# The rows of 14 of 16 experts fetched by an indirect DMA from a copy of x in HBM, and the next gate product set between up and down

## The chip, the core and the metric

The kernel runs on one core of a Trainium2 chip. The metric is the time of one execution in device microseconds (us); the median of three runs stands for the kernel. The core's engines work side by side, each through its own list of instructions in order: TensorE (PE in the profile, with its weight loads as PEld) does matrix products and transposes, VectorE (DVE) and ScalarE (ACT) work on rows of 128 partitions, GpSimd (POOL) does a little of the same and can issue DMAs whose addresses come from a tile, SyncE (SP) issues the plain loads. An engine whose next instruction waits for a semaphore holds up everything behind it in its list.

## What is computed

An encoder of two layers on 512 tokens of 1024 channels, all in float32. A layer adds the outputs of four mixers to x, then those of a mixture of 16 experts in which each expert chooses its own 64 tokens:

```python
def expert_choice_moe(x, w_router, w_gate, w_up, w_down):
    b, L, d = x.shape
    cap = EC_CAPACITY * L // N_EXPERTS
    aff = jax.nn.softmax((x @ w_router).astype(F32), axis=-1)
    gate, idx = lax.top_k(jnp.swapaxes(aff, 1, 2), cap)
    xe = jax.vmap(lambda xb, ib: xb[ib])(x, idx)
    hdn = jax.nn.silu(jnp.einsum("becd,edf->becf", xe, w_gate)) * jnp.einsum("becd,edf->becf", xe, w_up)
    ye = jnp.einsum("becf,efd->becd", hdn, w_down) * gate[..., None].astype(x.dtype)
    return jax.vmap(lambda ib, yb: jnp.zeros((L, d), yb.dtype).at[ib.reshape(-1)].add(yb.reshape(-1, d)))(idx, ye)
...
        x = x + mix @ w_out[l]
        x = x + expert_choice_moe(rmsnorm(x, norm_ffn_w[l]), router_w[l], moe_w_gate[l],
                                  moe_w_up[l], moe_w_down[l])
```

The change lies in this last line alone, the "expert stage" below, which runs once in each layer.

## The kernel before

x lies in SBUF as four tiles of 128 tokens (`xrow(t)`). The three matrices of an expert are 1024 by 1024 float32, 4 MB each, 201 MB in a layer. They come as pieces of 512 KB (8 for a matrix), issued by SP in the order gate, up, down (`pieces`, L1351) into the slots of several tile pools that are used in turn (`ring`); a piece is issued once the product that read the slot's last piece is done, so SP waits for PE as well as for old DMAs. Some 40 pieces are there when the stage begins.

For each expert `ranks` transposes the 512 affinities onto every partition (`er`, L1278) and counts on DVE for each token how many are above it (`egt`, four instructions, L1282). `choose` (L1290, four on DVE) turns the ranks into a 0/1 matrix `eselr` of 512 tokens by 64 places, scaled by one over the root of the token's mean square. `expert_tokens` multiplies that matrix with x on PE (`ex`, L1301: 8 instructions, 16 matmul records in the trace since a float32 instruction leaves two), copies the result on ACT (`exe`, L1304), transposes it (`exT`, L1308, and DVE L1310, where the norm's weight is put on), builds the unscaled matrix `esel` on DVE (L1313) and from it the 64 gate values (`ers`, L1317, and DVE `erg`, L1320).

The products are `eg` and `eu` (gate and up: `exT` against the weights), and `ey` (down), all on L1359, 16 instructions or 32 records each. The hidden rows are silu(`eg`) on ACT (`eh`, L1406) times `eu` on DVE (L1409); they are transposed on PE (`ehT`, L1415) and copied by ACT (L1417), which `ey` waits for. ACT and DVE scale `ey` by the gate in two parts (`eY`, L1428 and L1429). Once for every two experts, `combine` puts the 128 rows back in their places by a product with the transposed choice (`eoT`, L1374, `eot` on ACT, `ec`, L1385) and adds them into new tiles of x (L1387).

The code is written expert by expert: `eg`, `eu`, then the next expert's rows (`prep`), `ehT`, `ey`, `combine`. A scheduler then sets the order on each engine, so that neighbouring steps can be mixed.

Of the kernel before, what the change touches and what calls it, by code (L numbers as in the profile page):

```python
# [20 lines left out]
P = 128  # L21
# [14 lines left out]
C_ID, C_LE, C_GE, C_IOTA, C_N = 0, 128, 256, 384, 448  # L36


def shape_constants():
# [6 lines left out]
    c[:, C_IOTA:C_IOTA + 64] = np.arange(1, 65)  # L46
    same = (p[:, None] // 32) == (p[None, :] // 32)
# [4 lines left out]
    # times n = c + 4 j of the classes c; frequencies w = 2 pi (f + 1/2) / 2 L, f < 128, stand for four:  # L52
    # w, pi - w, pi / 2 - w, pi / 2 + w
# [52 lines left out]
def encoder(ctx: ExitStack, tc: tile.TileContext, d, out, dbg=None, stages=None, nlayers=NL):  # L106
# [44 lines left out]
    def slots_in_order():  # L151
        """The tiles of a tag take their slots in program order."""
        last, seen = {}, set()
        for ins in list(nc.cur_bb.bb.instructions):
            for o in ins.outs:
                ap = getattr(o, "bass_ap", None)
                n = ap.tensor.name if ap is not None else None
                if n in made and n not in seen:
                    seen.add(n)
                    tag = made[n]  # L160
                    if tag in last and last[tag] is not ins:
                        no_sync(ins, last[tag], "slots in program order")
                    last[tag] = ins
# [16 lines left out]
    # ---------------------------------------------------------------- constants  # L180
# [38 lines left out]
    def masks():  # L219
# [5 lines left out]
        # of tokens of the same affinity the earlier one goes first: a bound for differences, by place  # L225
# [4 lines left out]
    # ------------------------------------------------- per-channel parameters  # L230
# [59 lines left out]
    def squares(ss, x, junk, both=False):  # L290
        """Sums of squares of the halves of a row into ss."""
# [8 lines left out]
    def row_rstd(ss, name):  # L300
        """One over the roots of the mean squares of the rows of ss."""
# [68 lines left out]
    def proj_cm(hT, raw, c, pool=False):  # L370
        """128 columns from c of raw, channels on partitions -> PSUM bank [128, 512]."""
# [10 lines left out]
    def proj_tm(l, hT, pieces, use, pool=False, raws=()):  # L382
        """Columns of pieces [(c0, n)], tokens on partitions; use(t, psum bank)."""
# [26 lines left out]
    def weave(*streams):  # L410
        """Emits streams (weight, generator) side by side, each yield being a part of the weight."""
# [14 lines left out]
    def silu_inplace(x, e, dst):  # L426
        """x: clamped at FLOOR; e: scratch of the same shape; dst = x*sigmoid(x)."""
# [10 lines left out]
    def mix_put(m, i, src, w=None):  # L438
        """src: [128 channels, 512] of mixer m, tile i, scaled by column w."""
# [8 lines left out]
    # ------------------------------------------------------------------- hyena  # L448
# [32 lines left out]
    def filter_hidden(cols, spec, zT, ws, w3, fb):  # L481
        """The first layer's spectrum; what the second's is made of (on partitions 64..) into scratch. A generator."""
# [32 lines left out]
    def filter_spec(spec, h, w3, fb, dec, kt):  # L515
        """The spectrum of a layer's filters into spec. A generator."""
# [14 lines left out]
        # sp[:, m, i]: frequencies w and pi - w (f = 0), pi / 2 - w and pi / 2 + w (f = 1); i: real part and  # L531
        # imaginary part, the latter with the other sign for pi - w and pi / 2 - w
# [57 lines left out]
    def hyena(l, st, spec):  # L590
# [4 lines left out]
        # cosine and sine sums of the classes; of those the spectra (xs as the filters', sine sums)  # L595
# [17 lines left out]
        def quarter(lo, hi, b):  # L613
            """lo = hi turned forth by b, hi = hi turned back; cosine and sine parts."""
# [16 lines left out]
        # what gives the samples of the classes  # L631
# [23 lines left out]
    # ------------------------------------------------------------------- mamba  # L655
# [45 lines left out]
    def mamba(l, st, bc, cols):  # L701
# [29 lines left out]
        # the cumulative sums in three exact bfloat16 parts, transposed: row 8*t + c of a part  # L731
# [35 lines left out]
        # states of the chunks and their scan  # L767
# [30 lines left out]
        # C B^T of every chunk, transposed; one bank for each group  # L798
# [78 lines left out]
    # --------------------------------------------------------------- attention  # L877
# [130 lines left out]
    # ------------------------------------------------------------------- HGRN2  # L1008
# [28 lines left out]
    def hgrn_values(v):  # L1037
        """The values of a chunk of 32 tokens, alone in the chunk's columns among those of 64 tokens."""
# [60 lines left out]
    def hgrn(l, st, cols, lb):  # L1099
# [25 lines left out]
                # R[:, n, c]: the state after chunk c (in the direction's order)  # L1125
# [60 lines left out]
    # ------------------------------------------------------------------ output projection  # L1186
# [10 lines left out]
    def out_part(t, n, js, W):  # L1197
        """Channel tiles js [(mixer, k)] of the mixers into the rows t, columns of half n."""
# [17 lines left out]
    def out_last(l, m, W):  # L1216
        """The first channel tile of mixer m; the halves of its weights into W. A generator."""
# [8 lines left out]
    # ------------------------------------------------------- expert choice MoE  # L1226
# [9 lines left out]
    def router(rw, st):  # L1236
        pl = bank_b("rl")
        plv = pl[:, :64].rearrange("p (t e) -> p t e", t=4)
        ra = small([4, 1 + NE], "ra")
        mx = small([4], "rmx")  # L1240
        den = small([4], "rden")
        for t in range(4):
# [12 lines left out]
            for k in range(8):  # L1255
                T.matmul(plv[:, t], xs[k // 4][:, k % 4], rw[:, k], start=(k == 0), stop=(k == 7))
            V.reduce_max(mx[:, t:t + 1], plv[:, t], axis=AX.X)
            V.tensor_scalar(ra[:, t, 1:], plv[:, t], mx[:, t:t + 1], None, op0=ALU.subtract)
# [5 lines left out]
            rsqrt(ra[:, t, 0:1], ss[:, 0:1], D, "ffn")  # L1264
            A.activation(ra[:, t, 1:], ra[:, t, 1:], AF.Exp, scale=ra[:, t, 0:1], accum_out=den[:, t:t + 1])
            V.reciprocal(den[:, t:t + 1], den[:, t:t + 1])
            V.tensor_scalar(ra[:, t, 1:], ra[:, t, 1:], den[:, t:t + 1], KEY, op0=ALU.mult, op1=ALU.mult)
# [3 lines left out]
    SELR = (V, V, V, V)  # L1271

    def ranks(e, ra, selr=None):
        """The ranks of the tokens, from one, by their affinity to expert e. The affinities are scaled by KEY:
        the difference of two that are not the same is then above TIE."""
        pr = bank_b("er")
        for t in range(4):
            T.transpose(pr[:, t * P:(t + 1) * P], ra[:, t, 1 + e:2 + e].to_broadcast([P, P]), ident)  # L1278
        rk = small([4], "erk", bufs=2)
        g = page([L], "egt", BF)  # L1280
        for c in range(4):
            V.scalar_tensor_tensor(g, pr, ra[:, c, 1 + e:2 + e], tie[:, 384 - c * P:896 - c * P],  # L1282
                                   op0=ALU.subtract, op1=ALU.is_gt, accum_out=rk[:, c:c + 1])
            if selr is not None:
                choose(selr, rk, ra, c, SELR[c])
# [6 lines left out]
    def expert_tokens(e, ra, nw, rk, sel, selr):  # L1292
        """The 64 tokens of expert e: their normed rows, transposed, and their gates; their choice into sel."""
        if selr is None:
            selr = page([4, 64], "eselr")
            for t in range(4):
                choose(selr, rk, ra, t, V)
        px = bank_b("ex")
        for t in range(4):
            for h in range(2):  # L1300
                T.matmul(px[64 * h:64 * h + 64], selr[:, t], xrow(t)[:, h * 512:(h + 1) * 512],  # L1301
                         start=(t == 0), stop=(t == 3))
        xe = page([L], "exe")
        A.activation(xe, px, AF.Copy)  # L1304
        yield
        pt = bank_b("exT")
        for j in range(4):
            T.transpose(pt[:, j * P:(j + 1) * P], xe[:, j::4], ident)  # L1308
        xeT = page([4, 2, 64], "exT")
        V.tensor_mul(xeT, pt.rearrange("p (j h s) -> p j h s", j=4, h=2), nw[:, :, :, None].to_broadcast([P, 4, 2, 64]))  # L1310
# [8 lines left out]
        gate = small([1], "erg", bufs=2)  # L1319
        V.tensor_scalar(gate, pr[:, :1], 1.0 / KEY, None, op0=ALU.mult)  # L1320
        yield xeT, gate

    # pieces of the experts' matrices go round the slots of all the tags
# [5 lines left out]
    def pieces(l, view):  # L1329
        """A generator: loads one piece after the other."""  # L1330
        spare = []
        for e in range(NE):
            for m in ("gate", "up", "down"):
                rows = d["moe_w_" + m][l, e].rearrange("(h p j) f -> h p j f", h=2, p=P)
                v = view[e, m] = []
# [214 lines left out]
```

## Time and profile before

| what | value |
|---|---|
| three runs | 1733.29 to 1740.3 us, median 1737.68 us |
| span of the profiled execution | 1732.9 us |
| median less span | 4.8 us |
| PE busy | 1643.3 us, 95% of the span |
| weights' and other plain loads (queue q1) | 455.10 MB |
| expert stage, first layer | first `eg` at 372 us, last `ey` ends at 861 us |
| expert stage, second layer | first `eg` at 1225 us, last `ey` ends at 1714 us |

The profile shows one execution of one core; what lies around its span can only be seen from the median, 4.8 us. The two expert stages are 489 us each, 56% of the span together, and look alike, so one of them is read here and counted twice. A matmul's end is modelled, so that a busy PE need not be at its peak; idle time of an engine that nobody waits for costs nothing.

### The profile page before, as it was taken

What the parts mean: (1) busy time and instruction counts of PE and PEld (TensorE: products, weight loads), DVE (VectorE), ACT (ScalarE), POOL (GpSimd) and SP (SyncE); (2) the same over time, 40 slices, a digit from 0 to 9 for tenths busy, and PEclk for the clock granted to TensorE, in tenths of its full rate; (3) what the DMA queues carried; (4) which work ended last, traced back from release to release, by engine and by line L of the source; (5) the groups of instructions that cost most, each with busy time, mean ns of one, the idle gap of its engine ahead of it and who ended that gap; (6) DMA issues with size and microseconds to landing.
All of it is one profiled execution on the core that took longest, in us unless ns stands there. A gap on an engine that the chain in (4) does not pass through costs nothing.

```text
span 1732.9 us, 23297 instructions
## 1 busy us (share of the span) xinstructions
PE 1643.3 (95%) x9155; PEld 935.1 (54%) x9155; DVE 812.5 (47%) x1785; ACT 421.7 (24%) x849; POOL 166.8 (10%) x158
## 2 busy tenths in 40 slices
PE   7989999989999999999989999899999999999996
PEld 6778777754344333433368787787343343334332
DVE  6677776642334233233165767856332333233233
ACT  4343424321011111111252444344111011111103
POOL 3132131000000000000033223300000000000001
PEclk9989999999999999999989889999999999999998
DMA  5411126659999999999413111286699999999981
GB/s 171 112 49 50 50 73 237 254 210 375 381 409 411 410 411 410 411 407 396 143 50 97 50 42 57 74 308 231 234 376 411 411 411 410 411 411 408 409 329 49
DMA packets 150959, 457.03 MB, mean 264 GB/s; under 512 B 19928, under 2 KB 56184, under 8 KB 142658
## 3 DMA queue, kind: packets, MB, share of 16 engines
q1 hardware_dynamic: 145606, 455.10, 68.4%
q8 instruction: 72, 1.18, 0.3%
q10 hardware_dynamic: 5244, 0.45, 0.2%
q14 instruction: 37, 0.30, 0.1%
HBM read 453.25 MB, written 2.24 MB: 263 GB/s over the span
## 4 chain that ended last, share of the span: by engine, by line
PE 85%; DVE 7%; ACT 3%; issue 3%; POOL 2%; DMA 1%; SPq 0%; DVEq 0%; ACTq 0%; POOLq 0%
PE eg L1359 14%; PE ey L1359 13%; PE eu L1359 13%; PE ex L1301 7%; PE ec L1385 3%; PE pcm L377 3%; PE pcm L378 3%; PE pcm L379 3%; PE po L1202 2%; PE po L1203 2%; PE po L1204 2%; PE ptm L400 2%; PE ptm L399 1%; PE ptm L401 1%; PE ehT L1415 1%
## 5 line engine op out<-in xcount | busy, mean ns | idle before, releaser
L1359 PE MATMUL eu<-we,exT 128*64 128x512 f32 x1024 | 280.2, 593 | 0.0
L1359 PE MATMUL eg<-we,exT 128*64 128x512 f32 x1024 | 252.3, 596 | 1.6 <-DVE exT L1310 1.6
L1359 PE MATMUL ey<-we,ehT 128*64 128x512 f32 x1024 | 247.4, 598 | 3.5 <-ACT ehT L1417 3.5
L1301 PE MATMUL ex<-x,eselr 128*64 128x512 f32 x512 | 178.0, 615 | 2.6 <-DVE eselr L1290 2.6
L1429 DVE SCALAR_TENSOR_TENSOR eY<-ey,erg,eY 64x512 fp32r<-64x512 f32 x64 | 48.0, 749 | 263.1 <-ACT eY L1428 262.7
L1409 DVE TENSOR_TENSOR eh<-eh,eu 128x512 f32<-128x512 f32 x32 | 22.0, 687 | 313.1 <-PE eu L1359 313.1
L1359 PEld LDWEIGHTS eu<-we,exT 128*64 128x64 f32 x1024 | 90.4, 137 | 135.9 <-issue 128.6
L1359 PEld LDWEIGHTS eg<-we,exT 128*64 128x64 f32 x1024 | 75.1, 137 | 143.4 <-issue 128.8
L1359 PEld LDWEIGHTS ey<-we,ehT 128*64 128x64 f32 x1024 | 73.8, 137 | 117.9 <-issue 102.4
L379 PE MATMUL pcm<-hT,whl 128*128 128x512 f32 x320 | 129.4, 405 | 3.5 <-DVE whl L363 3.5
L378 PE MATMUL pcm<-hT,whl 128*128 128x512 f32 x320 | 131.1, 410 | 0.0
L377 PE MATMUL pcm<-hT,whl 128*128 128x512 f32 x320 | 130.7, 408 | 0.0
L1428 ACT ACTIVATE eY<-ey,erg 64x512 fp32r<-64x512 f32 x64 | 43.7, 683 | 231.8 <-PE ey L1359 209.9
L1282 DVE SCALAR_TENSOR_TENSOR egt<-er,ra,tie 128x512 bf16<-128x512 f32 x128 | 95.8, 748 | 4.3 <-PE er L1278 1.8
L1301 PEld LDWEIGHTS ex<-x,eselr 128*64 128x64 f32 x512 | 54.5, 142 | 76.2 <-issue 65.7
L1387 DVE TENSOR_TENSOR x<-x,ec 128x512 f32<-128x512 f32 x128 | 80.6, 682 | 14.8 <-PE ec L1385 14.3
L362 POOL TENSOR_SCALAR wtm<-wraw 128x1024 fp32r<-128x1024 f32 x16 | 22.8, 1427 | 648.9 <-PE ec L1385 595.1
L1304 ACT ACTIVATE exe<-ex 128x512 f32<-128x512 f32 x32 | 19.1, 597 | 261.1 <-PE ex L1301 261.1
L1406 ACT ACTIVATE eh<-eg 128x512 f32<-128x512 f32 x32 | 19.1, 597 | 259.6 <-PE eg L1359 259.6
L399 PE MATMUL ptm<-wtm,hT 128*128 128x256 f32 (+1 forms) x256 | 75.3, 296 | 1.7 <-DVE aqs L906 1.7
L1385 PE MATMUL ec<-eY,eot 128*128 128x512 f32 x256 | 70.2, 410 | 4.7 <-DVE eY L1429 2.8
L400 PE MATMUL ptm<-wtm,hT 128*128 128x256 f32 (+1 forms) x256 | 73.4, 289 | 1.4 <-DVE wtm L363 1.3
(381 smaller groups left out, 2500.2 us busy)
## 6 DMA issues: line engine op xcount, KB each, us to landing
we<-in_moe_w_gate_dram SPq DMA_DIRECT2D x216, 512.0 KB
we<-in_moe_w_down_dram SPq DMA_DIRECT2D x216, 512.0 KB
we<-in_moe_w_up_dram SPq DMA_DIRECT2D x208, 512.0 KB
wraw<-in_w_in_dram SPq DMA_DIRECT2D x27, 1024.0 KB
we<-in_moe_w_up_dram SPq DMA_DIRECT2D x24, 1024.0 KB
we<-in_moe_w_gate_dram SPq DMA_DIRECT2D x20, 1024.0 KB
we<-in_moe_w_down_dram SPq DMA_DIRECT2D x20, 1024.0 KB
wo<-in_w_out_dram SPq DMA_DIRECT2D x8, 1024.0 KB
```

What stands on the lines that cost most here:

```text
L377: T.matmul(ps, w[:, 0, k, :], H[k], start=(k == 0), stop=False)
L378: T.matmul(ps, w[:, 0, k, :], Lo[k], start=False, stop=False)
L379: T.matmul(ps, w[:, 1, k, :], H[k], start=False, stop=(k == 7))
L399: T.matmul(dst, h, w[:, 0, k % 4], start=(k == 0), stop=False)
L400: T.matmul(dst, h, w[:, 1, k % 4], start=False, stop=False)
L1282: V.scalar_tensor_tensor(g, pr, ra[:, c, 1 + e:2 + e], tie[:, 384 - c * P:896 - c * P], op0=ALU.subtract, op1=ALU.is_gt, accum_out=rk[:, c ...
L1301: T.matmul(px[64 * h:64 * h + 64], selr[:, t], xrow(t)[:, h * 512:(h + 1) * 512], start=(t == 0), stop=(t == 3))
L1359: T.matmul(ps[f][64 * f:64 * f + 64], xT[:, j, h], qs[4 * h + j][:, f * 512:(f + 1) * 512], start=(h == 0 and j == 0), stop=(h == 1 and j ...
L1385: T.matmul(ps, ot[:, t * P:(t + 1) * P], Y[i][q][n], start=(q == 0), stop=(q == 1))
L1387: V.tensor_add(dst, xrow(t)[:, c] if first else dst, ps)
L1428: A.activation(hi, src, AF.Copy, scale=gate[c])
L1429: V.scalar_tensor_tensor(lo, src, gate[c], hi.bitcast(F32), op0=ALU.mult, op1=ALU.subtract)
```

## The change

`router` writes each tile of x, as soon as it is complete, to a DRAM tile `xd` by a DMA of ACT's queue (four of 512 KB in a layer), where a token is two rows of 512 channels. The tile `ra` now holds three numbers for each token and expert: affinity, one over the root, and the row's place. One product, `ers` (64x3 instead of 64x1), yields for the 64 chosen tokens all three at once. DVE makes the integer row numbers (`erow`) and gate and root (`erg`) of them, and POOL issues one indirect DMA that brings the 128 half rows of 2 KB, 256 KB, into `exe`. ACT scales `exe` in place by the root. Experts 0 and 1 keep the product `ex`.

An iteration is now: up of e; scale and transpose the rows of e+1; ranks, choice and fetch of e+2; gate of e+1; transposed hidden rows of e; down of e; every second time the combine. The pieces are loaded in that order too (gate 0, up 0, gate 1, down 0, up 1, ...). The combine adds into the old tiles of x, so that four tiles of pool H come free: H gives 7 pieces in every turn, where it gave 8, 3 or 4, less one tile for `ra`.

```diff
-    def choose(selr, rk, ra, t, eng):
-        """The choice among the tokens of tile t, scaled by one over their roots."""
-        eng.tensor_scalar(selr[:, t], iota, rk[:, t:t + 1], ra[:, t, 0:1], op0=ALU.is_equal, op1=ALU.mult)
...
+    def expert_choice(e, ra, rk, sel):
         o = 64 * (e % 2)
         for t in range(4):
             V.tensor_scalar(sel[:, t, o:o + 64], iota, rk[:, t:t + 1], None, op0=ALU.is_equal)
         pr = bank_b("ers")
         for t in range(4):
             for h in range(2):
-                T.matmul(pr[64 * h:64 * h + 64, :1], sel[:, t, o:o + 64].bitcast(F32), ra[:, t, 1 + e:2 + e],
+                T.matmul(pr[64 * h:64 * h + 64, :3], sel[:, t, o:o + 64].bitcast(F32), ra[:, t, e],
                          start=(t == 0), stop=(t == 3))
+        row = small([1], "erow", I32, bufs=2)
+        V.tensor_scalar(row, pr[:, 2:3], pk[:, C_HALF:C_HALF + 1], None, op0=ALU.add)
+        gr = small([2], "erg", bufs=4)
+        V.tensor_mul(gr, pr[:, :2], pk[:, C_KEY:C_KEY + 2])
+        return gr, row
...
+    def rows_fetched(xd, row):
+        xe = tl("E", [L], "exe")
+        G.indirect_dma_start(xe, None, xd, bass.IndirectOffsetOnAxis(ap=row, axis=0))
+        return xe
...
+            load(xd[2 * P * t:2 * P * (t + 1)].rearrange("(p h) d -> p (h d)", h=2), xrow(t))
...
+        order = [(0, "gate")]
         for e in range(NE):
-            for m in ("gate", "up", "down"):
+            order += [(e, "up"), (e + 1, "gate"), (e, "down")]
...
         for e in range(NE):
-            xeT, gate = nxt
-            if e + 1 < NE:
-                rk = ranks(e + 1, ra)
...
+            up(e)
+            if e + 1 < NE:
+                if e:
+                    A.activation(xe, xe, AF.Copy, scale=choice[e + 1][0][:, 1:2])
+                cols_[e + 1] = expert_columns(xe, nw)
+            if e + 2 < NE:
+                choose(e + 2, ranks(e + 2, ra))
+                xe = rows_fetched(xd, choice[e + 2][1])
             if e + 1 < NE:
+                gate(e + 1)
+            down(e, hidden_columns(e))
...
-                    dst = new[0][t][:, c]
-                    V.tensor_add(dst, xrow(t)[:, c] if first else dst, ps)
+                    V.tensor_add(xrow(t)[:, c], xrow(t)[:, c], ps)
...
-        ring[:] = LATE + FIRST + ["H"] * 3 + EARLY + LATE
+        ring[:] = LATE + FIRST + ["H"] * 7 + EARLY + LATE
```

What the scheduler makes of it shows on PE first. Before, around the rows of expert 5 (`ex_4387`), PE's list in the middle of an up product, `eu_4361`, of expert 4 (the row at the end starts its down product):

```order
L1301 MATMUL ex_4387<-x_90,eselr_4382 64x512
L1359 MATMUL eu_4361<-we_4327,exT_4248 64x512 x2
L1301 MATMUL ex_4387<-x_90,eselr_4382 64x512
L1301 MATMUL ex_4387<-x_91,eselr_4382 64x512
L1359 MATMUL eu_4361<-we_4329,exT_4248 64x512 x2
L1359 MATMUL eu_4361<-we_4331,exT_4248 64x512 x2
L1301 MATMUL ex_4387<-x_91,eselr_4382 64x512
L1301 MATMUL ex_4387<-x_92,eselr_4382 64x512 x2
L1301 MATMUL ex_4387<-x_93,eselr_4382 64x512 x2
L1415 MATMUL ehT_4398<-pk,eh_4378 128x128 x4
L1308 MATMUL exT_4405<-pk,exe_4396 128x128 x4
L1359 MATMUL ey_4427<-we_4333,ehT_4403 64x512 x2
```

Now, PE's list in the gate product `eg_4244` of expert 5, from the ranks of expert 6 (`er_4213`) to the transposes of its fetched rows (`exT_4358<-pk,exe_4242`):

```order
L1286 MATMUL er_4213<-pk,ra_3226 128x128 x4
L1376 MATMUL eg_4244<-we_4186,exT_4211 64x512 x2
L1304 MATMUL ers_4229<-ra_3226,esel_4224 64x3 x2
L1409 MATMUL ehT_4275<-pk,eh_4089 128x128 x4
L1376 MATMUL eg_4244<-we_4246,exT_4211 64x512
L1304 MATMUL ers_4229<-ra_3226,esel_4224 64x3 x2
L1376 MATMUL eg_4244<-we_4246,exT_4211 64x512 x2
L1304 MATMUL ers_4229<-ra_3226,esel_4224 64x3 x4
L1376 MATMUL eg_4244<-we_4246,exT_4211 64x512
L1376 MATMUL eg_4244<-we_4248,exT_4211 64x512 x4
L1376 MATMUL eg_4244<-we_4251,exT_4211 64x512 x2
L1332 MATMUL exT_4358<-pk,exe_4242 128x128 x4
```

The eight `ex` instructions are gone, `ers` has moved from the down product to the gate product right behind `er`, and between the last `ers` (from which the row numbers come) and the transposes of the rows fetched by them stand 7 instructions of `eg`. For the other even experts from 2 to 14 it is 9 with four `ehT` (experts 2 and 4), 7 (14) or 6 (8, 10 and 12). For the odd experts from 3 to 15 a whole `ey`, a combine and 10 to 16 `eu` stand between, but only 7 to 13 `eg`, with `ehT` and `eoT`, up to the end of the gate product. On ACT, before, around the rows of expert 4 (`exe_4041`, `ex_4032`):

```order
L1406 ACTIVATE eh_4023<-eg_3989 128x512
L1304 ACTIVATE exe_4041<-ex_4032 128x512
L1417 ACTIVATE ehT_4048<-ehT_4043 128x512
L1428 ACTIVATE eY_3925<-ey_4072,erg_3906 64x512
L1376 ACTIVATE eot_4098<-eoT_4093 128x512
```

And now, from the scaling of expert 7's fetched rows (`exe_4393`) on; `eg_4395` is the gate product of expert 6, `ehT_4430` belongs to the hidden rows of expert 5, `ey_4437` is its down product:

```order
L1456 ACTIVATE exe_4393<-exe_4393,erg_4391 128x512
L1396 ACTIVATE eh_4428<-eg_4395 128x512
L1411 ACTIVATE ehT_4435<-ehT_4430 128x512
L1432 ACTIVATE eot_4473<-eoT_4468 128x512
L1424 ACTIVATE eY_4315<-ey_4437,erg_4052 64x512
L1424 ACTIVATE eY_4316<-ey_4437,erg_4052 64x512
```

The silu used to stand ahead of the row copy and belonged to the same expert as the `ehT` behind it; now the scaling of the fetched rows stands first, then the silu of the next expert's gate product, and then the `ehT` copy for the down product that follows.

## Rows read from the trace of the kernel before

**Rows 1.** The page: span, PE's busy time, DMA share in 40 slices.

```profile
span 1732.9 us, 23297 instructions
PE 1643.3 (95%) x9155; PEld 935.1 (54%) x9155; DVE 812.5 (47%) x1785; ACT 421.7 (24%) x849; POOL 166.8 (10%) x158
DMA  5411126659999999999413111286699999999981
```

**Rows 2.** Windows, two experts each: length, busy by engine, PEclk, DMA share, GB/s.

```profile
401.00:461.10 60.10, 60.07 (x303) 24.22 (x304) 19.84 (x50) 6.99 (x12) 0.00 (x0) 1.00 0.98 385
461.10:521.20 60.10, 60.07 (x302) 24.22 (x304) 19.84 (x50) 6.94 (x12) 0.00 (x0) 1.00 1.02 412
521.20:583.24 62.04, 60.90 (x302) 25.23 (x304) 19.92 (x50) 6.35 (x11) 0.00 (x0) 1.00 1.02 410
583.24:646.92 63.68, 61.45 (x302) 24.58 (x300) 19.93 (x50) 6.91 (x11) 0.00 (x0) 1.00 1.03 410
646.92:710.61 63.69, 61.45 (x303) 24.59 (x300) 19.93 (x50) 6.91 (x11) 0.00 (x0) 1.00 1.02 412
710.61:774.28 63.67, 61.43 (x303) 26.75 (x300) 19.92 (x50) 6.91 (x11) 0.00 (x0) 1.00 1.02 408
774.28:837.00 62.72, 60.49 (x299) 24.16 (x296) 19.93 (x50) 6.91 (x11) 0.00 (x0) 1.00 0.87 345
837.00:861.20 24.20, 22.61 (x105) 7.35 (x100) 2.19 (x3) 4.44 (x6) 0.00 (x0) 1.00 0.36 113
```

**Rows 3.** The chain that ended last, early experts: start, length, what.

```profile
363.89 6.05 PE ex L1301 x16
...
414.91 3.43 PE ex L1301 x16
...
461.10 7.02 PE eg L1359 x32
```

**Rows 4.** The same chain in a late expert, end of an up product.

```profile
697.50 2.59 PE eu L1359 x11
...
700.18 0.70 DVE eh L1409
...
700.93 0.75 PE ehT L1415 x4
```

**Rows 5.** Groups: row copy, silu, hidden rows' copy, ranks; choice, gate: min/median/max ns.

```profile
L1304 ACT ACTIVATE exe<-ex 128x512 f32<-128x512 f32 x32 | 19.1, 597 | 261.1 <-PE ex L1301 261.1
L1406 ACT ACTIVATE eh<-eg 128x512 f32<-128x512 f32 x32 | 19.1, 597 | 259.6 <-PE eg L1359 259.6
L1417 ACT ACTIVATE ehT<-ehT 128x512 f32<-128x512 f32 x32 | 19.1, 597 | 78.9 <-PE ehT L1415 78.0
L1282 DVE SCALAR_TENSOR_TENSOR egt<-er,ra,tie 128x512 bf16<-128x512 f32 x128 | 95.8, 748 | 4.3 <-PE er L1278 1.8
...
L1313 DVE TENSOR_SCALAR esel<-pk,erk x128: 243/249/255, 372.0 to 1667.5; 128x64 fp32r<-128x64 f32 x128
...
L1320 DVE TENSOR_SCALAR erg<-ers x32: 146/154/160, 373.7 to 1682.9; 128x1 f32<-128x1 f32 x32
```

**Rows 6.** The issue of a DMA on ACT's queue: min/median/max ns.

```profile
L172 ACTq DMA_DIRECT2D rw<-in_router_w_dram x2: 697/707/717, 58.2 to 63.0; - x2
```

**Rows 7.** The chain between the layers: first loads of the second, their first product.

```profile
854.21 7.74 DMA wraw<-in_w_in_dram
...
884.61 0.12 PE ptm L399
```

**Rows 8.** Loads from issue to use: timeline of `hm`, chain for pk and dft.

```profile
39.69 0.36 SPq L1480 DMA_DIRECT2D hm<-in_c_hmask_dram  x1
41.83 0.85 POOL L1481 TENSOR_SCALAR hmask<-hm 128x256 uint8<-128x256 int32 x1 [2.66 <-DMA hm<-in_c_hmask_dram]
...
1.65 5.11 DMA pk<-in_c_pack_dram
...
1086.09 7.86 DMA dft<-in_c_dft_dram
```

More of the change, by code (lines that the diff above doesn't have):

```diff
@@ L46, in shape_constants @@
     c[:, C_IOTA:C_IOTA + 64] = np.arange(1, 65)
+    c[:, C_TOK:C_TOK + 4] = 2 * (P * np.arange(4)[None, :] + p[:, None])
+    c[:, C_HALF] = p >= 64
+    c[:, C_KEY] = 1.0 / KEY
+    c[:, C_KEY + 1] = 1.0
     same = (p[:, None] // 32) == (p[None, :] // 32)
@@ L1281, in ranks @@
         for c in range(4):
-            V.scalar_tensor_tensor(g, pr, ra[:, c, 1 + e:2 + e], tie[:, 384 - c * P:896 - c * P],
+            V.scalar_tensor_tensor(g, pr, ra[:, c, e, 0:1], tie[:, 384 - c * P:896 - c * P],
                                    op0=ALU.subtract, op1=ALU.is_gt, accum_out=rk[:, c:c + 1])
             if selr is not None:
-                choose(selr, rk, ra, c, SELR[c])
+                V.tensor_scalar(selr[:, c], iota, rk[:, c:c + 1], ra[:, c, e, 1:2], op0=ALU.is_equal, op1=ALU.mult)
         return rk
-    def choose(selr, rk, ra, t, eng):
-        eng.tensor_scalar(selr[:, t], iota, rk[:, t:t + 1], ra[:, t, 0:1], op0=ALU.is_equal, op1=ALU.mult)
[L1292 to L1310, printed above, removed]
+    def expert_choice(e, ra, rk, sel):
         o = 64 * (e % 2)
@@ L1360, in expert_mm, with moe, choose, need @@
                              start=(h == 0 and j == 0), stop=(h == 1 and j == 3))
-    def moe(l, ra, nw, load_next, view):
-        Y, sels = {}, {}
-        new = [None]
-        def prep(e, rk, selr=None):
+    def moe(l, ra, nw, load_next, view, xd):
+        Y, sels, choice, cols_, hid = {}, {}, {}, {}, {}
+        def choose(e, rk):
             if e % 2 == 0:
                 sels[e // 2] = page([4, P], "esel", F32R)
-            return expert_tokens(e, ra, nw, rk, sels[e // 2], selr)
+            choice[e] = expert_choice(e, ra, rk, sels[e // 2])
+        def need(e, m):
+            while len(view.get((e, m), [])) < 8:
+                next(load_next)
+            return view[e, m]
+        def gate(e):
+            ps = bank_a("eg")
+            expert_mm([ps] * 2, cols_[e], need(e, "gate"))
+            hs = hid[e] = page([L], "eh")
+            silu = A.activation(hs, ps, AF.Silu)
+            if e == NE - 1:
+                act_set(LNEXP, silu)
+        def up(e):
+            ps = bank_a("eu")
+            expert_mm([ps] * 2, cols_.pop(e), need(e, "up"))
+            V.tensor_mul(hid[e], hid[e], ps)
+        def hidden_columns(e):
+            hs = hid.pop(e)
+            pt = bank_b("ehT")
+            for j in range(4):
+                T.transpose(pt[:, j * P:(j + 1) * P], hs[:, j::4], ident)
+            hT = page([4, 2, 64], "ehT")
+            A.activation(hT, pt.rearrange("p (j h s) -> p j h s", j=4, h=2), AF.Copy)
+            return hT
+        def down(e, hT):
+            py = [bank_a("ey"), bank_b("ey")] if e == NE - 1 else [bank_a("ey")] * 2
+            expert_mm(py, hT, need(e, "down"))
+            i, o = e // 2, 64 * (e % 2)
+            if e % 2 == 0:
+                Y[i] = [[page([L], "eY", F32R) for _ in range(2)] for _ in range(2)]
+            g = choice.pop(e)[0]
+            for n in range(2):
+                c, src = slice(64 * n, 64 * n + 64), py[n][64 * n:64 * n + 64]
+                hi, lo = (Y[i][q][n][o:o + 64] for q in range(2))
+                A.activation(hi, src, AF.Copy, scale=g[c, 0:1])
+                V.scalar_tensor_tensor(lo, src, g[c, 0:1], hi.bitcast(F32), op0=ALU.mult, op1=ALU.subtract)
         def combine(i):
@@ L1376, in combine @@
             A.activation(ot, pt, AF.Copy)
-            first = new[0] is None
-            if first:
-                new[0] = [tl("H", [D], "x") for _ in range(4)]
             for t in range(4):
@@ L1395, in moe @@
+        selr = [page([4, 64], "eselr") for _ in range(2)]
+        rk = [ranks(0, ra, selr[0])]
+        cols_[0] = expert_columns(rows_by_product(0, selr[0]), nw)
+        rk.append(ranks(1, ra, selr[1]))
+        gate(0)
+        choose(0, rk[0])
+        xe = rows_by_product(1, selr[1])
+        choose(1, rk[1])
         for e in range(NE):
-            xeT, gate = nxt
+            up(e)
             if e + 1 < NE:
-                rk = ranks(e + 1, ra)
-            while len(view.get((e, "down"), [])) < 8:
-                next(load_next)
@@ L1401, in moe @@
-            pg_ = bank_a("eg")
-            expert_mm([pg_] * 2, xeT, view[e, "gate"])
-            pu = bank_a("eu")
-            expert_mm([pu] * 2, xeT, view[e, "up"])
-            hs = page([L], "eh")
-            silu = A.activation(hs, pg_, AF.Silu)
-            if e == NE - 1:
-                act_set(LNEXP, silu)
-            V.tensor_mul(hs, hs, pu)
-            if e + 1 < NE:
-                nxt = prep(e + 1, rk)
-                next(nxt)
-            pt = bank_b("ehT")
-            for j in range(4):
-                T.transpose(pt[:, j * P:(j + 1) * P], hs[:, j::4], ident)
@@ L1504, in encoder @@
         st = []
-        route = router(fc[l][1], st)
+        xd = dp.tile([2 * L, L], F32, name=f"xd{l}")
+        route = router(fc[l][1], st, xd)
         for t in range(4):
@@ L1514, in encoder @@
             ra, = st
-            show(f"aff{l}", ra[:, :, 1:])
-            X[:], rows = moe(l, ra, fc[l][0], load_next, view)
+            rows = moe(l, ra, fc[l][0], load_next, view, xd)
     final_norm(rows)
```

104 lines of the change are left out of this document (52 added, 52 removed).

## Prediction

> **What bounds the kernel now.** I read the page first: PE is busy for 95% of the span, and the slices of the two expert stages show DMA at nine tenths or more as well [rows 1]. Two engines close to full means that a stage must be read by itself. The windows of two experts do that [rows 2]: until 521 us a pair of experts takes 60.1 us with PE busy for all of it, so there PE is the bound. From 521 us a pair takes 62.0 to 63.7 us and PE idles for 1 to 2.2 us of it, while the loads run at 408 to 412 GB/s. A pair's weights are 6 matrices of 4.19 MB, 25.17 MB, and at 411 GB/s they need 61.2 us. So PE and the stream of weights are within 4% of each other all the way, and PE ends last: by the share of the stretch 774 to 837 (345 of 411 GB/s over 62.72 us) the stream is through at about 827 us, 34 us before the last down product ends at 861. Work taken off PE shortens the stage, but only until PE catches up with the stream.
>
> Last I read what the chain is made of. A row product `ex` costs 3.43 us (6.05 for the first one, which stays) and a weight product 7.02 us or 0.44 for one of its 16 instructions [rows 3]. In late experts the end of an up product is followed by a stop: `eu` ends at 700.09, DVE multiplies until 700.88, and only then `ehT` starts [rows 4].
>
> **The change part by part**, for one layer, then twice. The sum is made against the profiled span of 1732.9; what lies around it, 4.8 us to the median, stays.
>
> *Removed.* 14 of 16 `ex`: 14 x 3.43 = 48.0 us [rows 3]. The copies `exe` on ACT become scalings of the same shape (597 ns), no difference. The `choose` instructions leave DVE, which nobody then waits for.
>
> *Moved, to the good.* With a gate product between up and `ehT`, the DVE multiplication of rows 4 is covered. I take the pairs' excess over the early 60.1 us as what such stops cost now: 1.9 + 3.6 + 3.6 + 3.6 + 2.6 = 15.3 us [rows 2]. Both ends: nothing, if they come back elsewhere, and 15.3.
>
> *Moved, to the bad.* (1) The row numbers need the ranks, and `ers` now stands 3.0 us of PE work (5 `eg` at 0.44, four `ehT` at 0.19 [rows 3, 4]) behind `er`. DVE needs 4 x 0.748 + 4 x 0.249 = 4.0 us for ranks and choice [rows 5], and some 0.2 us for the transposes' multiplication ahead of them. PE waits about 1.2 us, 14 times: 17 us. Before, `ers` stood in the down product, long after. (2) `ey` needs the ACT copy `ehT`, which now stands behind the silu of a gate product that ends directly before `ey`: 0.60 + 0.60 [rows 5] and three handings over of 0.05 to 0.1 [rows 4], 1.45 us, 15 times: 22 us. (3) In the router four DMA issues of ACT, 0.7 us each [rows 6], and some copies on DVE; only those of the last tile lie on the path: 1.5 us, at most 3 if all four did. The 2 MB that they write are spread over the router, where nothing waits for loads; nothing else of this layer follows on SP's or POOL's list that they would hold up. The queue of POOL is otherwise empty in this stage [rows 2]. Accumulating in place and 7 slots of H instead of 8, 3 or 4 I cost at nothing: PE, not SP, is late. The last pieces lie in slots that the next layer's loads (`wraw`) want, which now wait for the last `ey`: issued at 861 instead of 854, they land 7.74 us later, while the first product of them, `ptm`, starts at 884.61 [rows 7]. That is covered by 15 us of combine and norm.
>
> *Added: the fetch.* Call L the time from POOL's issue until the rows can be used. Around it lie `erow` (0.15), the scaling (0.60) and handings over (0.25), 1.0 us [rows 4, 5]. For the even experts the order leaves 6 to 9 instructions of `eg` as cover: 4.7, 4.7, 3.1, 3.1, 2.6, 2.6 and 2.6 us, 3.4 on average. So PE stands for L + 1.0 - 3.4 at each of 7 fetches: 7 L - 16.5 us. For the odd experts the transposes come 20 us later, but ACT's list holds: silu and `ehT` are behind the scaling, which waits for the fetch. Up to the end of the gate product there are about 5.0 us, so from L = 4.0 on `ey` is late by L - 4.0, 7 times.
>
> The sum of a layer: 17 + 22 + 1.5 - 16.5 - 48.0 - 15.3 + 7 L = 7 L - 39.3, and 7 (L - 4.0) more above 4.0. Zero is at L = 4.8.
>
> *L itself.* No POOL DMA stands in the trace. From below: `hm`, 128 KB on quiet queues, can be used 2.14 us after its issue began [rows 8]. With 256 KB at 411 GB/s that is 2.14 + 0.32 = 2.5 us. If the weights' queue keeps half of the DMA engines, the transfer takes 1.28 instead of 0.32 us and L is 3.1. From above: `pk`, 224 KB, the nearest in size, behind 1 MB of other loads, 5.11 us; `dft`, 512 KB in traffic, 7.86 us [rows 8]. The fetch has its own queue but shares the engines with weights at 411 GB/s, and POOL first works out 128 addresses, for which there is no row. I take 4.3, a little above the middle of 3.1 and 5.11. The fetched 256 KB also take 0.64 us each from the stream: 9 us a layer, hidden as long as PE is behind the stream.
>
> The Trainium skill, page "DMA: Bandwidth & Descriptors", section "Anatomy of one DMA — SWDGE (gpsimd) path", gives a DMA from POOL about 2.0 us and its bytes at 436 GB/s; worked out from it, L is an estimated 2.6 us, and the sum -21.1 us a layer, 1695 us in all. No row here can show it.
>
> At L = 4.3: 30.1 - 39.3 + 2.1 = -7.1 us a layer, -14.2 in both: a span of 1718.7, and 1723 us by the median.
>
> **The rivals.** *Fast: the fetch is short and the stream becomes the bound.* With L = 2.5 the sum is -21.8 a layer, 1694 us. The stream stops that at about the same place: it now ends near 827, the fetches add 9, and a down product of 6.9 must follow, 843 instead of 861, -18 a layer, 1701 us; lower only if SP, no longer waiting for PE, issues sooner. For it: quiet loads are as short as 2.1 us. Against: the queues are at 411 GB/s just here. *No difference:* L of 4.5 to 5.1, within 0.5% of 1738, which is about what a measurement can tell from no change; `pk`'s 5.11 gives +4.2 a layer, 1746 us. *Slower: the fetch is late and holds ACT.* From L = 4.8 on each fetch costs more than its share of the saving, at even experts on PE itself, at odd ones because ACT's list waits with silu and `ehT` behind the scaling. L = 6.0 gives +16.7 a layer, 1771; `dft`'s 7.86 gives +42.7, 1823. For it: both loads measured in traffic are over 5 us. Against: those two stood behind other loads in one queue. *A variant of it:* DVE holds up POOL while it writes its addresses. DVE's choices `esel` run from SBUF to SBUF beside it, but behind `erow` stand only a few of them, so I give it 1 in 20; 2.5 us more at each fetch is L = 6.8, +27.9 a layer, 1794 us. The Trainium skill, page "SBUF — State Buffer", section "SBUF: two separate sides", names such a lock and measured 0.62 us becoming 3.1; no run here shows it.
>
> **How the numbers follow.** L from 3.1 to 4.5, 1702 to 1729 us: 0.36, the likeliest, with the forecast of 1723 in it. Fast, 1690 to 1702: 0.12. No difference, 1729 to 1746: 0.19. Slower, 1746 to 1823: 0.33, the late fetch 0.28 and the lock 0.05. So faster 0.48, same 0.19, slower 0.33. Cases of both signs hold much of the chance, so beside the likeliest one's own 1702 to 1729 stands the range from 1690 (the stream's bound with SP a little earlier) to 1782 (L of 6.4); above it lies about 0.1, below it less.
>
> **What would show it.** The time from POOL's issue to ACT's scaling is L; PE's idle time before `exT` of even experts should be L - 2.4, about 2 us. `ey` should wait 1.5 us for ACT's `ehT`, `ers` about 1.2 us for DVE. `ex` should fall from 32 groups to 4. A pair should take near 61 to 62 us in all stretches, with loads above 405 GB/s and the stream's end nearer to the last `ey`. I am wrong if PE waits for pieces of weights instead (then the stream is the bound and L did not matter), if ACT stands at the scaling for more than 5 us after POOL's issue, or if the clock falls below 1.00 in the stops, which are longer than today's.

## The result, and the profile after

The changed kernel takes 1825.0 us (median of 4, 1823.9 to 1831.3) where the kernel before, run beside it, takes 1736.7: 1.052 times the time, 95% interval 1.049 to 1.055. It is slower, by 88 us, where I had forecast a gain of 14; the time lies above the range. The page of the changed kernel: the span, PE's busy time, the granted clock and the loads in 40 slices, and the queue of POOL's DMAs, which is new:

```profile
span 1822.1 us, 22349 instructions
...
PE 1609.2 (88%) x8707; PEld 906.5 (50%) x8707; DVE 792.7 (44%) x1715; ACT 421.1 (23%) x849; POOL 193.9 (11%) x186
...
PEclk9989999999999899999989889999999989988998
...
GB/s 178 91 56 39 70 70 301 261 303 361 418 421 388 358 333 397 324 356 411 92 53 99 41 47 93 119 251 268 377 383 420 421 345 400 344 351 370 316 312 47
...
q0 software_dynamic: 2240, 7.34, 1.1%
```

PE is busy for 88% instead of 95% [rows 1]: the row products are gone, and idle time and a lower clock have taken more than their place. The loads fall below 400 GB/s in the middle of each stage, so the stream of weights is not the bound. The windows of two experts say the same (length, busy time by engine, PEclk, DMA share, GB/s):

```profile
406.46:466.35 59.89, 55.82 (x269) 22.93 (x269) 18.13 (x44) 6.81 (x12) 1.91 (x2) 0.97 0.97 373
466.35:527.65 61.30, 54.96 (x260) 21.98 (x260) 18.04 (x44) 6.91 (x11) 1.90 (x2) 0.96 1.02 421
527.65:599.83 72.18, 60.14 (x268) 22.33 (x269) 18.08 (x44) 6.83 (x11) 1.90 (x2) 0.93 0.99 400
...
670.38:743.09 72.71, 59.33 (x268) 22.20 (x269) 18.14 (x44) 6.83 (x11) 1.91 (x2) 0.92 0.92 355
```

The first two pairs, where the order leaves 9 `eg` instructions and four `ehT` as cover, take about what they took [rows 2]; from expert 6 on, with 6 or 7 instructions, a pair takes 71 to 73 us. What waits is in PE's list of waits (engine, line, waited for: us, times, longest) and in the group of the tile `exe`:

```profile
PE exT L1332 <- ACT exe L1456: 66.3, 14, 6.4
PE ey L1376 <- ACT ehT L1411: 57.1, 28, 4.4
PE ers L1304 <- DVE esel L1300: 14.1, 18, 1.6
...
DMA to landing us min/median/max: 4.7/6.5/7.1
```

L, the time that I had put at 4.3 us, is 6.5. One fetch of each kind, in the timeline of POOL and ACT (start, length, what, idle before and its releaser). For expert 8 POOL issues at 592.55, ACT can scale at 599.06; for expert 9 at 626.58, and ACT scales at 633.20, then does the silu that had been ready, and only then the copy that the down product waits for:

```profile
592.55 0.95 POOL L1326 DMA_INDIRECT exe<-xd,erow  x1 [35.95 <-DVE erg L1309]
626.58 0.95 POOL L1326 DMA_INDIRECT exe<-xd,erow  x1 [33.09 <-DVE erg L1309]
...
599.06 0.72 ACT L1456 ACTIVATE exe<-exe,erg 128x512 f32<-128x512 f32 x1 [24.50 <-DMA exe<-xd,erow]
...
633.20 0.72 ACT L1456 ACTIVATE exe<-exe,erg 128x512 f32<-128x512 f32 x1 [17.41 <-DMA exe<-xd,erow]
633.95 0.60 ACT L1396 ACTIVATE eh<-eg 128x512 f32<-128x512 f32 x1
634.44 0.59 ACT L1411 ACTIVATE ehT<-ehT 128x512 f32<-128x512 f32 x1
```

On PE these two stops look so (windows again, around the first and around the second; the first number behind the length is PE's busy time, the clock stands third from the end):

```profile
592.00:599.80 7.80, 2.16 (x12) 0.45 (x6) 0.00 (x0) 0.72 (x1) 0.95 (x1) 0.87 1.03 420
599.80:606.50 6.70, 5.42 (x18) 2.05 (x18) 0.00 (x0) 1.08 (x2) 0.00 (x0) 0.65 0.52 178
606.50:613.40 6.90, 6.90 (x32) 2.34 (x34) 0.00 (x0) 0.00 (x0) 0.00 (x0) 1.00 0.87 272
632.00:635.00 3.00, 0.00 (x0) 0.00 (x0) 0.00 (x0) 1.77 (x4) 0.00 (x0) 1.00 1.04 436
635.00:639.00 4.00, 3.91 (x12) 1.17 (x14) 0.00 (x0) 0.52 (x2) 0.00 (x0) 0.57 1.01 428
639.00:643.70 4.70, 4.70 (x24) 1.55 (x21) 0.00 (x0) 0.00 (x0) 0.00 (x0) 1.00 1.01 427
```

PE stands for about 5.6 us before 599.8, and for all of 632 to 635, and right after each stop it works at a mean granted clock of 0.65 and 0.57, near the lower of its two levels (1.2 instead of 2.4 GHz), for 4 to 7 us. The first costs 6.7 x 0.35 = 2.3 us more, the second 4.0 x 0.43 = 1.7.

So the theory: the fetch takes 6.5 us beside the stream; even experts pay for it on PE before the transposes, odd ones through ACT's list before the down product, and each stop is paid a second time by the clock. Rivals: the new order is what is slow; the fetched bytes disturb the stream; the clock has no part in it.

### The profile page after: what moved, and what is told of

The parts are those of the page before. It is cut to its first block, busy times and chain, and to the rows that moved or that the text cites. A ratio compares the mean times of both kernels' runs of the same rounds, so it can differ in the third digit from the quotient of the medians.

```text
span 1822.1 us, 22349 instructions
## 1 busy us (share of the span) xinstructions
PE 1609.2 (88%) x8707; PEld 906.5 (50%) x8707; DVE 792.7 (44%) x1715; ACT 421.1 (23%) x849; POOL 193.9 (11%) x186
## 5 line engine op out<-in xcount | busy, mean ns | idle before, releaser
L1376 PE MATMUL ey<-we,ehT 128*64 128x512 f32 x1024 | 251.3, 646 | 57.4 <-ACT ehT L1411 57.1
L1376 PE MATMUL eg<-we,exT 128*64 128x512 f32 x1024 | 283.8, 627 | 3.6 <-DVE exT L1334 3.6
L1376 PE MATMUL eu<-we,exT 128*64 128x512 f32 x1024 | 248.9, 596 | 0.0
L1326 POOL DMA_INDIRECT exe<-xd,erow x28 | 26.9, 962 | 1122.1 <-DVE erg L1309 1055.8
L1376 PEld LDWEIGHTS eu<-we,exT 128*64 128x64 f32 x1024 | 74.7, 137 | 138.2 <-issue 124.4
L1456 ACT ACTIVATE exe<-exe,erg 128x512 f32<-128x512 f32 x28 | 20.2, 721 | 510.8 <-DMA exe<-xd,erow 510.8
L1376 PEld LDWEIGHTS eg<-we,exT 128*64 128x64 f32 x1024 | 80.6, 143 | 111.0 <-issue 96.4
L1332 PE MATMUL exT<-pk,exe 128*128 128x128 f32 x128 | 29.7, 358 | 67.6 <-ACT exe L1456 66.3
L403 PE MATMUL ptm<-wtm,hT 128*128 128x256 f32 (+1 forms) x256 | 75.7, 297 | 1.8 <-DVE aqs L910 1.8
L404 PE MATMUL ptm<-wtm,hT 128*128 128x256 f32 (+1 forms) x256 | 73.6, 289 | 1.4 <-DVE wtm L367 1.3
L405 PE MATMUL ptm<-wtm,hT 128*128 128x256 f32 (+1 forms) x256 | 72.8, 287 | 0.0
L383 PEld LDWEIGHTS pcm<-hT,whl 128*128 128x128 f32 x320 | 63.1, 197 | 18.5 <-DVE whl L367 3.9
L381 PEld LDWEIGHTS pcm<-hT,whl 128*128 128x128 f32 x320 | 63.2, 198 | 16.6 <-issue 3.4
```

The costliest lines, as they stand in the source:

```text
L381: T.matmul(ps, w[:, 0, k, :], H[k], start=(k == 0), stop=False)
L383: T.matmul(ps, w[:, 1, k, :], H[k], start=False, stop=(k == 7))
L403: T.matmul(dst, h, w[:, 0, k % 4], start=(k == 0), stop=False)
L404: T.matmul(dst, h, w[:, 1, k % 4], start=False, stop=False)
L405: T.matmul(dst, g, w[:, 0, k % 4], start=False, stop=(k == 7))
L1376: T.matmul(ps[f][64 * f:64 * f + 64], xT[:, j, h], qs[4 * h + j][:, f * 512:(f + 1) * 512], start=(h == 0 and j == 0), stop=(h == 1 and j ...
```

## The experiments

Every time given for a run is the median of its runs, 2 to 8 of them; the two versions without the stream and with plain loads ran once each. 1737 (1734 to 1737 in the three sets) is the kernel before, run beside them. Waits are those of PE, summed over both layers.

### A fast copy in place of the fetch

```diff
-        G.indirect_dma_start(xe, None, xd, bass.IndirectOffsetOnAxis(ap=row, axis=0))
+        G.tensor_scalar(xe, xrow(0)[:, :L], gr[:, 0:1], None, op0=ALU.mult)
```

> The changed kernel, but in place of the fetch POOL copies half of x's first tile into the same tile, one instruction of about 1 us that needs the same gate and root values; the rows of 14 experts are therefore not the chosen ones, which is the part left out. Nothing else moves. Theory (the wait for the fetch, 6.5 us at the median from issue to landing in the changed kernel, stops PE before the transposes of even experts and, through ACT's list, before the down product of odd ones, and the stops also let the clock fall): with 1 us in place of 6.5 the stops before the transposes are gone, the ones before the down product fall to 1.5 to 2 us, the granted clock is back at about 0.975, and the time is 1690 to 1710 us. Rival (the new order itself is what is slow): within 30 us of the changed kernel's 1825.

Measured: 1715.1 us (ratio to before 0.987, 0.984 to 0.991), 5 us above the expected range, but 110 us below the changed kernel: the new order alone does not make 1825. The copy takes 1.56 us, not 1, and one thing did not stay as it was. The scheduler sets the order on PE by its own estimate of how long a step takes; with a copy in place of the DMA it left only 2 instead of 6 `eg` instructions between `ers` and `exT` (experts 8 and 10), so some of the stops remained:

```profile
PE ey L1376 <- ACT ehT L1411: 32.0, 28, 2.7
PE exT L1332 <- ACT exe L1456: 14.9, 10, 2.0
```

In the changed kernel these two are 57.1 and 66.3.

### The fetch one product earlier

```diff
         for e in range(NE):
+            if e + 2 < NE:
+                choose(e + 2, ranks(e + 2, ra))
+                xn = rows_fetched(xd, choice[e + 2][1])
             up(e)
...
-            if e + 2 < NE:
-                choose(e + 2, ranks(e + 2, ra))
-                xe = rows_fetched(xd, choice[e + 2][1])
+            if e + 2 < NE:
+                xe = xn
```

> The changed kernel with ranks, choice and fetch of the expert after next moved ahead of the up product in the code, so that a whole gate and down product stand on PE between the row numbers and the transposes; every fetch and every byte stays. Theory (too little cover for the fetch): 1695 to 1715 us, time from issue to landing still 6 to 7 us, no stop of PE before the transposes, 1.5 to 2 us before each down product. Rival (the fetched bytes disturb the stream of weights): the time stays above 1780, and PE waits for weights. Rival (new order is slow): above 1780 as well, with the stops elsewhere.

Measured: 1700.7 us, ratio 0.979 (0.976 to 0.982), with the same 28 fetches of 256 KB, and the landing as late as before:

```profile
PE ey L1376 <- ACT ehT L1411: 39.2, 32, 2.7
...
DMA to landing us min/median/max: 5.9/6.5/7.8
```

The wait before `exT` is gone from the list, the loads run at 420 GB/s. So neither the bytes nor L as such are the loss, but that too little stood between the row numbers and the transposes: 124 us for moving two lines.

### The new order without the fetch

```diff
-                choose(e + 2, ranks(e + 2, ra))
-                xe = rows_fetched(xd, choice[e + 2][1])
+                sr = page([4, 64], "eselr")
+                choose(e + 2, ranks(e + 2, ra, sr))
+                xe = rows_by_product(e + 2, sr)
```

> The new order of products and loads, but the rows of all 16 experts by the product on PE, with no fetch (the copy of x is still written). Theory: no long stops, so the clock stays near 0.975, and the 48 us of row products in a layer come back, beside the waits of the new order (of PE for ranks in front of the product that gives the gates, 1 to 2 us for each expert): 1770 to 1800 us, slower than before by 2 to 3.5%, faster than the changed kernel. Rival (the order alone is the whole loss): 1825 or more. Rival (the order costs nothing, the loss is all fetch): within 10 us of before's 1737.

Measured: 1775.9 us, ratio 1.022 (1.019 to 1.025). The new order has a price of its own, 39 us; 49 of the 88 us come from the fetch in the place of the products. Only a part of the 39 is waiting: PE's idle time is 11 us longer than before, its busy time 28 us (1671.5 instead of 1643.3) for the same number of matmul records. What makes them take longer in this order is not shown.

### Idle products in the stop

```diff
                 xe = rows_fetched(xd, choice[e + 2][1])
+                pf = bank_b("fill")
+                for q in range(8):
+                    T.matmul(pf[64 * (q % 2):64 * (q % 2) + 64, :448], choice[e + 2][0][:, 0:1].to_broadcast([P, 64]),
+                             pk[:, :448], start=(q < 2), stop=(q > 5))
```

> The changed kernel with 8 idle products (64x448, stationary the gates, result never read) for each fetched expert, placed on PE right behind the product that gives the row numbers, that is inside the stop that follows: 28 x 8 x 0.375, about 84 us of PE work more. Theory with the clock as second cause (the stops of 4 to 7 us let the granted clock fall to half for some 5 us each time, about 40 us in all): the stops get shorter by what the work fills, so the work costs nearly nothing, and most of the clock's loss comes back: 1785 to 1810 us, mean granted clock above 0.96. Rival (the clock is no part of it, the stops alone are the loss): 1820 to 1840. Rival (PE's work is the bound): up to 1909.

Measured: 1766.3 us, 59 us less than the changed kernel with 224 products more on PE (448 records), outside the range of the expectation on the good side. The waits of PE that remain:

```profile
PE ey L1376 <- ACT ehT L1411: 20.5, 20, 2.7
...
PE exT L1332 <- ACT exe L1456: 4.1, 6, 1.1
```

Together 24.6 us, 98.8 less than the 123.4 of the changed kernel, for about 84 us of added work: 15 us saved by that account. The other 44 must come from elsewhere, and the mean granted clock has gone from 0.945 to 0.973; 0.028 of 1822 us is 51 us. That the clock is worth some 40 to 50 us of the 88 is the reading that fits; that work costs less than nothing here is shown by the time itself.

### No stream of weights

```diff
-        order = [(0, "gate")]
-        for e in range(NE):
-            order += [(e, "up"), (e + 1, "gate"), (e, "down")]
-        order.remove((NE, "gate"))
+        order = [(0, "gate"), (0, "up"), (0, "down"), (1, "gate")]
...
-            while len(view.get((e, m), [])) < 8:
-                next(load_next)
-            return view[e, m]
+            return view[0, m]
```

> The changed kernel, but only the first expert's three matrices (and some pieces of the next) are loaded in each layer; all 16 experts are multiplied with these, so the weights of 15 experts are what is left out, and with them the loads during the stage. PE's work and the fetches are unchanged. Theory A (the fetch is slow because its packets share the DMA engines and HBM with the stream of weights): from issue to landing 3 to 4 us instead of 6.5, the stops before the transposes shrink by about 3 us, 1700 to 1740 us. Theory B (the time is POOL's own, working out 128 addresses and the completion): 6 us or more as before, and the time stays near 1810 to 1825.

Measured: 3.3 us from issue to landing, as theory A has it, and 1638.2 us, far below both ranges. I had not thought of what else goes with the loads: PE waits for no weights, and the order came out with 9 `eg` and four `ehT` as cover at every even expert from 2 to 14, so the time cannot be read against the others. L can:

```profile
DMA to landing us min/median/max: 3.2/3.3/3.6
```

The DMA packets show where the rest of 6.5 us is. Without the stream the fetch issued at 540.23 has no packet until 541.8 and all 80 between 541.8 and 543.6; in the changed kernel the one issued at 592.55 has none until 596.7, while only the weights' queue q1 moves, and all 80 from 596.7 to 599 (queue: packets, MB, share of 16 engines; first the changed kernel, its two stretches, then this one):

```profile
q1 hardware_dynamic: 477, 1.75, 102.9%
...
q1 hardware_dynamic: 197, 0.71, 75.7%
q0 software_dynamic: 80, 0.26, 28.0%
```

```profile
q0 software_dynamic: 80, 0.26, 52.3%
```

The data themselves take little longer beside the stream. It is the first packet that comes 2.5 us later. The other fetches agree: at the median of 28 the first packet comes 4.1 us after the issue in the changed kernel and 1.7 here.

### Plain loads in place of the indirect ones

```diff
-        G.indirect_dma_start(xe, None, xd, bass.IndirectOffsetOnAxis(ap=row, axis=0))
+        if e % 2:
+            A.dma_start(xe, xd[:P])
+        else:
+            G.tensor_copy(row, row)
+            G.tensor_copy(xe[:, 0:1], row)
+            G.dma_start(xe, xd[:P])
```

> The changed kernel, but in place of the indirect fetch a plain load of the same 256 KB (128 rows of 2 KB, the first of the copy): for even experts issued by POOL behind an instruction that reads the row numbers, for odd ones by ACT's queue without waiting for them. The chosen rows are left out, not the bytes. Theory A (sharing with the stream of weights): all of them take about as long as the indirect ones, 5.5 to 7 us, on either queue. Theory B (POOL's address work): POOL's plain load 1.5 us or more shorter than the indirect fetch, and ACT's 3 to 4 us. Time: the odd experts' scaling no longer holds ACT, the even stops stay: 1770 to 1800 us under A, below 1750 under B.

Measured: 1797.7 us, in the range of theory A. POOL's plain loads land after 5.9 to 7.1 us, 6.8 at the median, so the 128 addresses are not it. Of ACT's 14, which have no landing in the profile, most were issued while the stream happened to stand. Two were issued into it and show the same delay, though POOL has no part in them; the one at 396.79 has no packet of its queue q10 until 400.2 and all 144 by 402.6:

```profile
396.79 0.33 ACTq L1327 DMA_DIRECT2D exe<-xd  x1
```

```profile
q1 hardware_dynamic: 393, 1.42, 102.5%
...
q1 hardware_dynamic: 204, 0.75, 75.9%
q10 hardware_dynamic: 144, 0.26, 28.4%
```

The other of the two, at 1279.25, has its first packet 3.5 us after the issue as well. One at 517.55, in a moment without weights, has its first after 1.0 us and all its packets through by 520.0. So, as far as these cases go, a DMA of another queue comes to its turn some 2.5 us later while the weights run at 420 GB/s, whichever engine issues it. Theory A stands. By what rule the queues take turns no run here shows.

### The hidden rows' copy ahead of the silu

```diff
+            hT = hidden_columns(e)
             if e + 1 < NE:
                 gate(e + 1)
-            down(e, hidden_columns(e))
+            down(e, hT)
```

> The changed kernel with one line moved: the hidden rows are transposed and copied by ACT before the next gate product's silu in the code, so that on ACT the copy for the down product no longer stands behind the scaling of the fetched rows. Theory (odd experts lose through ACT's list, even ones on PE itself): the stops before the down product vanish (57 us of waiting in the changed kernel, and the falls of the clock behind them), those before the transposes of even experts stay: 1735 to 1770 us. Rival (ACT's list is not what holds the down product): above 1800.

Measured: 1729.5 us, level with before (ratio 0.998, 0.996 to 1.000), a little below the expected range. What is left on PE are the even experts:

```profile
PE exT L1332 <- ACT exe L1456: 53.3, 10, 6.3
```

The waits before `ey` are gone. The four even experts fewer in this row (10 instead of 14) are experts 2 and 4 of each layer, whose transposes the scheduler now put behind a down and an up product, so not all of the 96 us is ACT's list.

### Both moves

> Both moves together: ranks, choice and fetch ahead of the up product, and the hidden rows' copy ahead of the next silu. Theory: neither stop is left, PE catches up with the stream of weights, which then is the bound: 1675 to 1690 us, PE waiting for weight pieces in places, loads at 420 GB/s until a few us before the last down product. Rival (the stops left in the early version, 39 us before the down products, are covered by the stream anyway): 1695 to 1705, no better than the early version's 1700.7.

Measured: 1672.7 us, ratio 0.964 (0.961 to 0.967): faster than both kernels, by 61 (against the runs beside it) and 152 us, and 2 us below the expected range. Three windows from its middle, PE's largest wait (both layers together), and the page's chain that ended last, by engine:

```profile
430.00:485.00 55.00, 54.90 (x278) 22.15 (x276) 18.13 (x44) 8.34 (x13) 1.90 (x2) 1.00 1.02 420
...
597.00:657.00 60.00, 55.77 (x261) 21.80 (x259) 18.14 (x44) 6.02 (x10) 1.91 (x2) 0.97 1.02 421
...
778.00:812.00 34.00, 33.73 (x150) 12.81 (x148) 7.93 (x12) 4.07 (x8) 0.00 (x0) 1.00 1.02 420
```

```profile
PE ers L1304 <- DVE esel L1300: 24.0, 10, 3.1
...
PE 84%; DVE 8%; ACT 3%; issue 2%; POOL 1%; DMA 1%; ACTq 0%; SPq 0%; DVEq 0%; POOLq 0%
```

The 39 us of waits in the early version were not covered by the stream: without them the time is 28 us lower. The loads stay at 420 GB/s to the last window, but they did so in the early version too, so this alone doesn't make the stream the bound. PE's list names no wait for weights, against the expectation (only its weight loads, PEld, wait for pieces, 58 times and for at most 0.6 us), and the chain that ended last has 1% of DMA. PE and the stream are nearly level here; that the stream is the bound is not shown.

### Both moves, without the fetch

The kernel of both moves with the third experiment's edit.

> Both moves of the fastest version, but the rows of all 16 experts by the product on PE, no fetch: what the fetch itself is worth once it is covered. Theory: without the fetch PE is the bound again, 14 products of 3.4 us in a layer come back and only what PE had to spare against the stream hides them: 1735 to 1770 us, no better than before's 1737 and 60 to 95 us above the version with the fetch. Rival (the stream of weights is the bound in both, the gain of the fast version comes from the order alone): within 15 us of 1673.

Measured: 1764.6 us, ratio to before 1.016 (1.012 to 1.019), 92 us above the same order with the fetch. The fetch is worth about what the prediction took for its products, 96 us, once its time is covered: PE's busy time differs by 95.0 us (1669.7 and 1574.7). The order alone gains nothing; it costs 29 us.

## Why the prediction was wrong

- **The step that failed is the value of L**: "I take 4.3, a little above the middle of 3.1 and 5.11". It is 6.5 us. The quiet fetch of the fifth run, 3.3 us, is 0.8 above the 2.5 that I had for quiet queues from `hm`, and the allowance for the stream was of the wrong kind: I let it halve the rate (0.96 us), while what it does is put off the first packet by 2.5 us and stretch the rest by some tenths. The two loads measured in traffic, 5.11 and 7.86 us [rows 8], have 6.5 half-way between them. The sign that I had named, ACT standing at the scaling for more than 5 us after POOL's issue, came. The Trainium skill's page "DMA: Bandwidth & Descriptors", section "Anatomy of one DMA — SWDGE (gpsimd) path", gave an estimated 2.6 us; both measured values are above it, and the measurement decides.
- **The sum itself, at the measured L**, gives 7 x 6.5 - 39.3 + 7 x 2.5 = 23.7 us a layer, +47 in both, 1785 us: the slow rival, which I had at 0.28, by its mechanism, both on PE and through ACT's list. In PE's list its waits are there, but not of the size that the sum has. `exT`: 2 x (7 x 6.5 - 16.5) = 58 us forecast, 66.3 measured. `ey` for ACT: 2 x (22 + 17.5) = 79 forecast, 57.1 measured. `ers` for DVE: 2 x 17 = 34 forecast, 14.1 measured. The products: 96 forecast, 95.0 of PE's busy time in the last two versions. The variant of this rival, DVE holding up POOL, is out: POOL's issue took 0.95 to 1.16 us in all 28 fetches, and without the stream, with DVE's work unchanged, L was 3.3.
- **The term that was missing is the clock.** "If the clock falls below 1.00 in the stops, which are longer than today's" stood among what would make me wrong, without a price. The windows show it after both kinds of stop, at 1.7 and 2.3 us for the two shown, and the run with idle products puts it at 40 to 50 us of the 88. The two pages part it from the waiting. The span grew by 89 us. PE's idle time (span less busy) grew by 123, from 89.6 to 212.9. PE's busy time fell by 34, from 1643.3 to 1609.2, where the products should have taken off 96: the rest of the work took 62 us longer. An estimate of the clock's part, from the trace, is half of PE's busy time at the lower level: 34 us before and 81 now, so 47 of the 62; with the idle products it is 35. The other 15 are not explained. At L = 6.5 the sum has 143 us more idle time (58 + 79 + 34 + 3, less 30.6 for today's stops), 20 more than came. So its 47 us fall short of 89 by the 62 that it had at nothing, less these 20.
- **Right** were the bound before, that PE and not SP would be late (the loads fall to 355 GB/s), and that the fetched bytes do no harm by themselves. The zero of the sum at L = 4.8 was not tested, and without the clock it is not to be trusted. The floor that I gave the stream, 1701 unless SP issues sooner, was too high: the fastest version takes 1673, with loads of 420 GB/s, not 411.
- **The forecast of the direction** rested on an unknown between 3.1 and 7.86 with the zero of the sum at 4.8 in between. The chance of 0.33 for slower was too small when the only two loads measured in traffic, both over 5 us, spoke for it.

## What to carry to other kernels

Before a fetch by computed addresses takes the place of work on the engine that is the bound, read in the order what stands between the moment the addresses are known and the first use, on the using engine and on every engine whose list the wait is put into; here 3 us stood there for a fetch of 6.5, and moving a few lines made +5.2% into -3.6%. This scheduler left 6 or 7 instructions of cover for the DMA at most even experts and 2 for a copy, by its own estimate, and that was too little beside a saturated stream; the fetch had to be issued earlier in the code by hand. And an instruction that waits for a DMA goes behind, not ahead of, whatever others are waiting for on that engine.

## What I had not expected of the hardware

- A DMA of 256 KB on a queue of its own takes 3.3 us from POOL's issue when nothing else is loaded and 6.5 us beside loads of 420 GB/s; 2.5 of the 3.2 us pass before its first packet. The two fetches of the changed kernel that came after the stream had thinned out landed after 4.7 and 5.0 us.
- 28 x 8 products whose result nobody reads made the kernel 59 us faster, with the granted clock at 0.973 instead of 0.945.
- A plain load issued by POOL is as slow as an indirect one, 6.8 against 6.5 us beside the stream.
